# Two weight blocks turned by the DMA crossbar, and a rewritten head, in a convolution with max pooling

## The chip, the cores and the metric

The kernel runs on one core of one Trainium2 chip. The time is device microseconds (us) of an execution. The profile shows one of these executions; its span is about 1.8 us shorter than the time quoted for the same run. Where a run is called slow, it was over 1.5% above the fastest run of the same kernel; ratios and intervals use fast runs alone.

## The reference

A 3x3 convolution with zero padding, followed by a 2x2 maximum. Cut to what matters:

```python
# x: (16, 64, 64, 64) float32, weight: (128, 64, 3, 3) float32, pool_size = 2
conv[b, co] += weight[co, ci, kh, kw] * x_pad[b, ci, kh:kh+h, kw:kw+w]
...
output[b, c, i, j] = max over the 2x2 window of conv[b, c]      # (16, 128, 32, 32) float32
```

## The kernel before

The sixteen images go through in 16 stages, each with a quarter (16 rows of the convolution, 8 of the pooled output) of two "k" images and of two "w" images. Both kinds use the fact that the two rows of a pooling window share a part of their sums: max(u+c, v+c) = max(u,v)+c. Seven combinations of the three weight rows are therefore made from the weights (blocks D2, G0, D0, G2, GM, G1, GP), and turned so that input channels lie on partitions, as TensorE needs them.

The steps have short names. For the k images: PA and PB are twelve products each on the rows themselves (`kx`), PR is six on sums of rows (`ks`) with G1. For the w images: P2 takes differences `we` with GM, P0 takes `wz` with G0, P3 takes `wy` with G2, P1 takes `ws` with GP, six products each. KS, WS, E, Z, Y make these rows (VectorE, or GpSimd for Z and Y). EV, MX, OD and CM copy out and take maxima; SE seeds an accumulator. TX turns block X on TensorE, VX copies it out of PSUM. The number after the point is the stage.

```python
    def turn(m):                                  # four TensorE transposes of one block
        t = free.popleft()
        turned[m] = t
        ...
        for j in range(lo, hi):
            nc.tensor.transpose(tp[...], wq[:, j : j + 2, :].rearrange("a b c -> a (b c)"), ident)

    def turn_out(m):                              # PSUM to the weights in SBUF
        ...
        if m == "GM":
            nc.scalar.mul(dst, src, 0.5)
        elif m == "GP":
            nc.vector.tensor_scalar_mul(out=dst, in0=src, scalar1=0.5)
        elif m in ("G0", "G1", "G2"):
            nc.scalar.copy(out=dst, in_=src)
        else:
            nc.vector.tensor_copy(out=dst, in_=src)
    ...
    def we(i):
        if i < 5:
            inst = on_vector(row_op(nc.vector, "we", i, 1, 0, SUB))
            if i == 0:
                behind(kload(0, chunk(2)[0], H), inst)     # GpSimd load of kx, with a cast
    ...
    def cast_rows(first):                          # XO, XE: kfirst to bf16
        inst = on_vector(nc.vector.tensor_copy(out=kx[0][:, first:khi:2, :], in_=kfirst[...]))
        if first == 1:
            for i in range(1, NQ):
                behind(wload(i), inst)             # SyncE loads wx1, wx2, wx3
    ...
    HEAD = """
        D2 g0 D0 g2 GS g1 TD2 VD2 TG0 VG0 XO TD0 VD0 TG2 VG2 TG1 VG1 XE GM PA.0 GP TGM VGM TGP
        KS.0 E.0 WS.0 PB.0 EV.0 X1 Z.0 Y.0 VGP P2.0 MX.0 SE.0 X2 PA.1 EV.1 WS.1 KS.1 E.1 PR.0
        P0.0 P3.0 Z.1 Y.1 OD.0 CM.0 P2.1 ev.0 PB.1 SE.1 mx.0 P0.1 P1.0 MX.1 P3.1 ev.1 od.0 PR.1
        ...
    """
    for n in range(8):                             # warm-up products on zeros
        warm = zero(n // 2, n % 2)
        if n == 3:
            behind(wload(0), warm)
            nc.sync.dma_start(out=ksecond, in_=rows_of(0, klo2, khi2))
```

Each engine works in the order in which its steps stand in the list. `wload(i)` is the load of the i-th quarter of the first w images; I call these loads wx0 to wx3.

Of the kernel before, what the change touches and what calls it, by code (L numbers as in the profile page):

```python
# [11 lines left out]
def kernel(  # L12
# [21 lines left out]
    nc = tc.nc  # L34
    FP32 = mybir.dt.float32
    BF16 = mybir.dt.bfloat16
    MAX = mybir.AluOpType.max
    ADD = mybir.AluOpType.add
    SUB = mybir.AluOpType.subtract

    B, CI, H, W = x.shape
# [4 lines left out]
    NQ = 4  # L46
# [13 lines left out]

    acc = [psum.tile([128, 2, R, W], FP32, name=f"acc_{i}") for i in range(4)]
    free = deque(range(4))
    unset = set()



# [3 lines left out]
    def behind(inst, other):  # L70
        if other is not None:
            tc.add_manual_dep(inst.ins, other.ins.name, SYNC, reason="order")

    def on_vector(inst):
        sbuf_op[0] = inst
        return inst

    def on_gpsimd(inst):
        behind(inst, sbuf_op[0])
        return inst  # L80


    def rows_of(p, lo, hi):
        return x[2 * p : 2 * p + 2].rearrange("b c h w -> (b c) h w")[:, lo:hi, :]

    def chunk(q):
        return (2 * R * q + (q > 0), min(H, 2 * R * (q + 1) + 1))
# [4 lines left out]
    def kload(j, lo, hi):  # L92
        if j not in kx:
            kx[j] = kx_pool.tile([128, H, W], BF16, name="kx")
        return nc.gpsimd.dma_start(out=kx[j][:, lo:hi, :], in_=rows_of(2 * j, lo, hi))  # L95

    def wload(i):
        j, q = divmod(i, NQ)
        lo, hi = chunk(q)
        return nc.sync.dma_start(  # L100
            out=wx[j % 2][:, lo + 1 : hi + 1, :], in_=rows_of(2 * j + 1, lo, hi)
        )
# [6 lines left out]
    klo2, khi2 = chunk(1)  # L109
    ksecond = const.tile([128, khi2 - klo2, W], FP32)  # L110
# [10 lines left out]
    D2, G0, D0, G2, GM, G1, GP = range(1, 29, 4)  # L121
    BLOCKS = {"D2": D2, "G0": G0, "D0": D0, "G2": G2, "GM": GM, "G1": G1, "GP": GP}
    wq = const.tile([CO, 29, CI], BF16)
    wt = const.tile([128, 28, CO], BF16)
# [4 lines left out]
    g0, g1, g2 = wv[:, 0:3, :], wv[:, 3:6, :], wv[:, 6:9, :]  # L129

    def slots(m):
        return wq[:, m : m + 3, :]

    def zero(t, h):
        return nc.tensor.matmul(  # L135
            acc[t][:, h], zeros[:, 0:128], zeros, start=True, stop=True, skip_group_check=True
        )

    turned = {}

    def turn(m):
        t = free.popleft()
        turned[m] = t
        unset.add(t)
        tp = acc[t][:, 0].rearrange("p a b -> p (a b)").bitcast(BF16)
        lo, hi = BLOCKS[m] - 1, BLOCKS[m] + 3
        for j in range(lo, hi):
            nc.tensor.transpose(  # L148
                tp[:, (j - lo) * 128 : (j - lo + 1) * 128],
                wq[:, j : j + 2, :].rearrange("a b c -> a (b c)"),  # L150
                ident,
            )

    def turn_out(m):
        t = turned[m]
        free.append(t)
        lo, hi = BLOCKS[m] - 1, BLOCKS[m] + 3
        src = acc[t][:, 0].rearrange("p a b -> p (a b)").bitcast(BF16)[:, 0 : (hi - lo) * 128]
        dst = wt[:, lo:hi, :].rearrange("p a b -> p (a b)")
        if m == "GM":  # L160
            nc.scalar.mul(dst, src, 0.5)
        elif m == "GP":
            nc.vector.tensor_scalar_mul(out=dst, in0=src, scalar1=0.5)
        elif m in ("G0", "G1", "G2"):
            nc.scalar.copy(out=dst, in_=src)
        else:
            nc.vector.tensor_copy(out=dst, in_=src)


    def taps(t, m0, rows, start=False, skip=None):  # L170
# [63 lines left out]
    def row_out(name, i):  # L234
        j, q = divmod(i, NQ)
        if (name, j) not in row:
            row[name, j] = row_pool.tile([128, HO, W], BF16, name=name)
        return row[name, j][:, q * R : (q + 1) * R, :]

    def row_in(t, first, pad):  # L240
        a = first + pad
        return t[:, a : a + 2 * R - 1 : 2, :]

    def row_op(engine, name, i, a, b, op):
        j, q = divmod(i, NQ)
        t, pad = (kx[j], 0) if name == "ks" else (wx[j % 2], 1)
        f = 2 * R * q
        return engine.tensor_tensor(  # L248
            out=row_out(name, i), in0=row_in(t, f + a, pad), in1=row_in(t, f + b, pad), op=op
        )  # L250

    def ks(i):
        on_vector(row_op(nc.vector, "ks", i, 0, 1, ADD))

    def ws(i):
        on_vector(row_op(nc.vector, "ws", i, 0, 1, ADD))
# [1 line left out]
    def we(i):  # L258
        if i < 5:
            inst = on_vector(row_op(nc.vector, "we", i, 1, 0, SUB))  # L260
            if i == 0:
                behind(kload(0, chunk(2)[0], H), inst)
        else:
            on_gpsimd(row_op(nc.gpsimd, "we", i, 1, 0, SUB))

# [69 lines left out]
    def cast_rows(first):  # L335
        inst = on_vector(
            nc.vector.tensor_copy(out=kx[0][:, first:khi:2, :], in_=kfirst[:, first:khi:2, :])
        )
        if first == 1:
            for i in range(1, NQ):  # L340
                behind(wload(i), inst)

    def cast_more(first):
        nc.scalar.copy(out=kx[0][:, klo2 + first : khi2 : 2, :], in_=ksecond[:, first::2, :])
# [2 lines left out]
        "g0": lambda: nc.scalar.copy(out=slots(G0), in_=g0),  # L347
        "g1": lambda: nc.scalar.copy(out=slots(G1), in_=g1),
        "g2": lambda: nc.scalar.copy(out=slots(G2), in_=g2),
        "D2": lambda: on_vector(nc.vector.tensor_sub(out=slots(D2), in0=g2, in1=g1)),  # L350
        "D0": lambda: on_vector(nc.vector.tensor_sub(out=slots(D0), in0=g0, in1=g1)),
        "GS": lambda: on_gpsimd(nc.gpsimd.tensor_tensor(out=gsum, in0=g0, in1=g2, op=ADD)),
        "GM": lambda: on_vector(
# [2 lines left out]
        "GP": lambda: on_vector(  # L356
            nc.vector.tensor_add(out=slots(GP), in0=gsum, in1=g1)
        ),
        "XO": lambda: cast_rows(1),
        "XE": lambda: cast_rows(0),  # L360
        "X1": lambda: cast_more(0),
        "X2": lambda: cast_more(1),
        "PA": pa, "PB": pb, "PR": pr, "P0": p0, "P1": p1, "P2": p2, "P3": p3,
        "KS": ks, "WS": ws, "E": we, "Z": wz, "Y": wy, "SE": seed,
        "EV": lambda i, h=None: evac(("k", i), h), "ev": lambda i, h=None: evac(("w", i), h),
        "MX": lambda i, h=None: rowmax(("k", i), h), "mx": lambda i, h=None: rowmax(("w", i), h),
# [3 lines left out]
    for m in BLOCKS:  # L370
        steps["T" + m] = lambda m=m: turn(m)
        steps["V" + m] = lambda m=m: turn_out(m)

    HEAD = """
        D2 g0 D0 g2 GS g1 TD2 VD2 TG0 VG0 XO TD0 VD0 TG2 VG2 TG1 VG1 XE GM PA.0 GP TGM VGM TGP
        KS.0 E.0 WS.0 PB.0 EV.0 X1 Z.0 Y.0 VGP P2.0 MX.0 SE.0 X2 PA.1 EV.1 WS.1 KS.1 E.1 PR.0
        P0.0 P3.0 Z.1 Y.1 OD.0 CM.0 P2.1 ev.0 PB.1 SE.1 mx.0 P0.1 P1.0 MX.1 P3.1 ev.1 od.0 PR.1
        WS.2 KS.2 E.2 Z.2 Y.2 OD.1 cm.0 CM.1 PA.2 EV.2 P2.2 PB.2 SE.2 mx.1 P1.1 P0.2 MX.2 P3.2
        od.1 ev.2 cm.1 E.3 KS.3 WS.3 Z.3 Y.3 PR.2 PA.3 OD.2 CM.2 P2.3 mx.2 EV.3 PB.3 SE.3 P1.2
# [12 lines left out]
    """  # L392
    FIRST, LAST = 4, 12

    for n in range(8):
        warm = zero(n // 2, n % 2)
        if n == 3:
            behind(wload(0), warm)
            nc.sync.dma_start(out=ksecond, in_=rows_of(0, klo2, khi2))
    kx[0] = kx_pool.tile([128, H, W], BF16, name="kx")  # L400

    def run(order):
# [44 lines left out]
```

## Time and profile before

| | before |
|---|---|
| time, median of 4 runs | 107.96 us (107.49 to 108.42) |
| profiled run, its span | 107.78 us, 106.0 us |
| TensorE products | 900: 8 warm-up, 28 transposes, 864 of the convolution |
| second we starts, P2.1 starts, PB.1 starts | 13.04, 13.77, 14.43 us |
| from PB.1 to the end of the block of products | 76.89 us (91.32 - 14.43) |

The page's slices cut the span into 40 parts of 2.65 us. A digit is the busy share in tenths, and PEclk the granted TensorE clock in tenths of full speed:

```profile
PE   5999999999999999999999999999999999999810
PEclk9999999999999999999999999999999999999998
```

TensorE has no hole and, once it is warm, no slice at a lower clock. One thing that the prediction did not show: what leads up to PB.1. The timeline of the head (start, length, engine, line, operation):

```profile
10.95 1.26 POOL L248 TENSOR_TENSOR wy<-wx 128x512 bf16<-128x512 f32 x1
11.10 1.68 DVE L248 TENSOR_TENSOR ws<-wx 128x512 bf16<-128x512 f32 x1
...
13.04 0.68 DVE L248 TENSOR_TENSOR we<-wx 128x512 bf16<-128x512 f32 x1
...
13.64 0.68 DVE L318 TENSOR_TENSOR o<-acc,od 128x512 f32<-128x512 f32 x1
...
14.43 1.46 PE L183 MATMUL acc<-kx,wt 64*128 64x512 bf16 x12
```

VectorE's second `ws` takes 1.68 us beside GpSimd's `wy`, although elsewhere it takes 0.68. The line at 13.64 is CM.0, which frees the accumulator that PB.1 needs. It ends at 14.32 and PB.1, the last line, starts at 14.43. So VectorE, too, runs nearly without slack here.

### The profile page before, as it was taken

The page shows a single profiled execution, that of the slowest core. Times are in us where ns is not written, and L with a number is a line of the kernel's source. Part 1 is how long each engine was busy: PE and PEld are TensorE (multiplying, and loading weights), DVE is VectorE, ACT ScalarE, POOL GpSimd, SP SyncE. Part 2 cuts the span into 40 slices and gives each one's busy share as a digit, 9 for nine tenths or more (in the row PEclk, how much of TensorE's full clock was granted, in tenths as well). Part 3 has the DMA queues.
Part 4 walks back from the last instruction along what each step waited for, and adds up shares of the span by engine and source line. Part 5 has one row for each costly group of instructions (what it writes and reads, how often), then busy time and mean ns, then how long its engine had stood idle before and what let it go on. Part 6 is the DMA issues. An engine that isn't in the chain of part 4 may idle for free.

```text
span 106.0 us, 2338 instructions
## 1 busy us (share of the span) xinstructions
PE 99.5 (94%) x900; PEld 46.0 (43%) x900; DVE 82.4 (78%) x113; ACT 72.8 (69%) x92; POOL 60.1 (57%) x69
## 2 busy tenths in 40 slices
PE   5999999999999999999999999999999999999810
PEld 2465434444444444444444444444444444455400
DVE  1398989979797868697887868687969878677950
ACT  4567985776767678767867676777777676775820
POOL 6205673924529494959567594949294856745000
PEclk9999999999999999999999999999999999999998
DMA  2999976999998569999959498999967412232052
GB/s 58 363 340 359 293 177 153 208 280 244 272 341 192 209 161 152 212 334 210 340 211 212 167 201 148 243 326 202 370 224 158 162 58 102 99 105 99 0 198 99
DMA packets 12475, 21.96 MB, mean 207 GB/s; under 512 B 944, under 2 KB 9136, under 8 KB 12464
## 3 DMA queue, kind: packets, MB, share of 16 engines
q1 hardware_dynamic: 11312, 18.03, 53.7%
q0 software_dynamic: 1008, 3.65, 20.0%
q8 instruction: 7, 0.11, 0.4%
q10 hardware_dynamic: 144, 0.13, 0.4%
q14 instruction: 4, 0.03, 0.1%
HBM read 17.07 MB, written 8.39 MB: 240 GB/s over the span
## 4 chain that ended last, share of the span: by engine, by line
PE 89%; DVE 6%; issue 1%; ACT 1%; DVEq 0%
PE acc L183 83%; DVE acc L299 5%; PE acc L135 3%; PE acc L148 2%; DVE o L318 1%; ACT od L304 1%; DVE zeros L112 0%; DVEq L299 0%
## 5 line engine op out<-in xcount | busy, mean ns | idle before, releaser
L183 PEld LDWEIGHTS <-wt 64*128 64x128 bf16 x864 | 42.6, 94 | 50.8 <-issue 1.1
L299 DVE TENSOR_TENSOR acc<-acc,ev 128x1024 f32<-128x1024 f32 (+1 forms) x34 | 39.6, 1166 | 12.3 <-PE acc L183 12.0
L183 PE MATMUL acc<-kx,wt 64*128 64x504 bf16 (+3 forms) x384 | 46.2, 373 | 0.0
L286 ACT COPY ev<-acc 128x1024 f32<-128x1024 f32 (+1 forms) x34 | 32.6, 964 | 12.5 <-PE acc L183 11.0
L248 POOL TENSOR_TENSOR wz<-wx 128x512 bf16<-128x512 f32 x16 | 20.4, 1273 | 30.2 <-DVE ws L248 23.3
L304 ACT COPY od<-acc 128x512 f32<-128x512 f32 x32 | 18.8, 587 | 11.5 <-PE acc L183 11.5
L318 DVE TENSOR_TENSOR o<-acc,od 128x512 f32<-128x512 f32 x32 | 21.9, 690 | 3.6 <-ACT od L304 3.6
L248 POOL TENSOR_TENSOR wy<-wx 128x512 bf16<-128x512 f32 x16 | 20.3, 1268 | 0.0
L295 ACT ACTIVATE acc<-acc 128x1024 f32<-128x1024 f32 x16 | 16.1, 1008 | 1.0 <-PE acc L183 0.6
L248 POOL TENSOR_TENSOR we<-wx 128x512 bf16<-128x512 f32 x11 | 14.0, 1276 | 0.1
L183 PE MATMUL acc<-ws,wt 64*128 64x504 bf16 (+1 forms) x96 | 13.0, 377 | 0.4 <-DVE acc L299 0.4
L183 PE MATMUL acc<-ks,wt 64*128 64x504 bf16 (+1 forms) x96 | 13.0, 377 | 0.1
L183 PE MATMUL acc<-we,wt 64*128 64x504 bf16 (+1 forms) x96 | 13.0, 377 | 0.0
L183 PE MATMUL acc<-wy,wt 64*128 64x504 bf16 (+1 forms) x96 | 13.0, 377 | 0.0
L183 PE MATMUL acc<-wz,wt 64*128 64x504 bf16 (+1 forms) x96 | 13.0, 377 | 0.0
L248 DVE TENSOR_TENSOR ws<-wx 128x512 bf16<-128x512 f32 x16 | 12.0, 747 | 0.0
L248 DVE TENSOR_TENSOR ks<-kx 128x512 bf16<-128x512 bf16 x16 | 6.7, 416 | 0.0
L95 POOL DMA_DIRECT2D kx<-in_x_dram x7 | 4.1, 591 | 3.5 <-DVE we L248 3.5
L135 PE MATMUL acc<-zeros 128*128 128x512 bf16 x8 | 3.6, 631 | 1.2 <-DVE zeros L112 1.2
L248 DVE TENSOR_TENSOR we<-wx 128x512 bf16<-128x512 f32 x5 | 3.4, 682 | 0.0
L148 PEld LDWEIGHTS <-wq 128*128 128x128 bf16 x28 | 2.4, 124 | 1.0 <-issue 0.6
L148 PE MATMUL acc<-ident,wq 128*128 128x128 bf16 x28 | 2.6, 265 | 0.0
(26 smaller groups left out, 14.9 us busy)
## 6 DMA issues: line engine op xcount, KB each, us to landing
out_dram<-o SPq DMA_DIRECT2D x31, 256.0 KB, 2.8
wx<-in_x_dram SPq DMA_DIRECT2D x8, 512.0 KB, 5.6
wx<-in_x_dram SPq DMA_DIRECT2D x4, 544.0 KB, 5.7
kx<-in_x_dram POOLq DMA_DIRECT2D x4, 496.0 KB, 7.7
wx<-in_x_dram SPq DMA_DIRECT2D x4, 480.0 KB, 4.7
kx<-in_x_dram POOLq DMA_DIRECT2D x3, 528.0 KB, 8.1
kfirst<-in_x_dram SPq DMA_DIRECT2D x1, 544.0 KB, 4.3
ksecond<-in_x_dram SPq DMA_DIRECT2D x1, 512.0 KB, 5.7
```

Source lines behind the costliest of these rows:

```text
L95: return nc.gpsimd.dma_start(out=kx[j][:, lo:hi, :], in_=rows_of(2 * j, lo, hi))
L135: return nc.tensor.matmul(acc[t][:, h], zeros[:, 0:128], zeros, start=True, stop=True, skip_group_check=True)
L148: nc.tensor.transpose(tp[:, (j - lo) * 128 : (j - lo + 1) * 128], wq[:, j : j + 2, :].rearrange("a b c -> a (b c)"), ident,)
L183: nc.tensor.matmul(dst[:, half, i0:i1, o0:o1], wt[lo : lo + CI, m0 + kw - half, :], rows(lo, i0, i1, c0, c1), start=start and kw == 1, sto ...
L248: return engine.tensor_tensor(out=row_out(name, i), in0=row_in(t, f + a, pad), in1=row_in(t, f + b, pad), op=op)
L286: nc.scalar.copy(out=ev[g][:, halves(h)], in_=acc[ta[g]][:, halves(h)])
L295: nc.scalar.mul(acc[t], acc[ta["w", i]], -1.0)
L299: nc.vector.tensor_tensor(out=t, in0=t, in1=ev[g][:, halves(h)], op=MAX)
L304: nc.scalar.copy(out=od[g][:, halves(h)], in_=acc[tb[g]][:, halves(h), :, 1::2])
L318: nc.vector.tensor_tensor(out=o, in0=acc[tb[g]][:, s, :, 0::2], in1=od[g][:, s], op=MAX)
```

## The change

The intent: take eight of the 28 weight transposes off TensorE (blocks G1 and GP) and give them to the DMA crossbar, which writes into the weights directly; start the convolution earlier with two warm-up products fewer; and issue each load only when its turn in the order of need has come, so that early loads have the DMA engines to themselves.

```diff
+    def turn_by_dma(m):
+        lo = BLOCKS[m] - 1
+        for j in (lo, lo + 1):
+            nc.sync.dma_start_transpose(
+                out=wt[:, j : j + 3 : 2, :], in_=wq[:, j : j + 4, :].rearrange("a b c -> a (b c)")
+            )
 ...
     def ks(i):
-        on_vector(row_op(nc.vector, "ks", i, 0, 1, ADD))
+        inst = on_vector(row_op(nc.vector, "ks", i, 0, 1, ADD))
+        if i == 0:
+            behind(kload(0, chunk(2)[0], H), inst)
 ...
             inst = on_vector(row_op(nc.vector, "we", i, 1, 0, SUB))
             if i == 0:
-                behind(kload(0, chunk(2)[0], H), inst)
+                for n in range(2, NQ):
+                    behind(wload(n), inst)
 ...
-        if first == 1:
-            for i in range(1, NQ):
-                behind(wload(i), inst)
+        if first == 0:
+            behind(wload(1), inst)
 ...
     HEAD = """
-        D2 g0 D0 g2 GS g1 TD2 VD2 TG0 VG0 XO TD0 VD0 TG2 VG2 TG1 VG1 XE GM PA.0 GP TGM VGM TGP
-        KS.0 E.0 WS.0 PB.0 EV.0 X1 Z.0 Y.0 VGP P2.0 MX.0 SE.0 X2 PA.1 EV.1 WS.1 KS.1 E.1 PR.0
+        D2 g0 D0 g2 GS g1 XG1 TD2 VD2 TG0 VG0 XO TD0 VD0 TG2 VG2 GM XE PA.0 TGM GP HGP XGP KS.0
+        PB.0 EV.0 VGM E.0 WS.0 X1 P2.0 Z.0 Y.0 SE.0 MX.0 X2 PA.1 EV.1 E.1 KS.1 WS.1 PR.0
         P0.0 P3.0 Z.1 Y.1 OD.0 CM.0 P2.1 ev.0 PB.1 SE.1 ...
-    for n in range(8):
+    for n in range(6):
```

Cut from the diff: ksecond's load now waits for the first difference block; all four accumulators start on the list of untouched ones, which have to be zeroed before they are seeded (e1 meets this); GM's scaling moves from ScalarE to VectorE (VGM, 0.42 us); GP is halved by ScalarE before it is turned (HGP). XG1 and XGP are two crossbar transposes each, issued by SyncE.

> **What bounds the kernel now.** I read the page's busy table first, then the chain that ended last in order of time, then the timeline of the first 22 us on every engine, then the DMA issues. The busy table, and the chain:
>
> ```profile
> PE 99.5 (94%) x900; PEld 46.0 (43%) x900; DVE 82.4 (78%) x113; ACT 72.8 (69%) x92; POOL 60.1 (57%) x69
> ```
>
> ```profile
> 0.86 0.28 DVE zeros L112
> ...
> 1.19 3.59 PE acc L135 x8
> 4.79 1.77 PE acc L148 x20
> 6.56 1.32 PE acc L183 x12
> 7.88 0.55 PE acc L148 x8
> 8.44 5.30 PE acc L183 x48
> 13.74 0.03 issue
> 13.77 77.56 PE acc L183 x720
> ```
>
> The columns are start, length and what ran. TensorE (PE) is the chain from 1.19 to 91.3 us almost without a hole. 720 convolution products take 77.56 us, 0.1077 us each, so all 864 need 93.05 us and cannot be shortened by this change. What is left of the 106.0 us span is 13 us: a head before 6.56 us (eight warm-up products, 3.59 us, and 20 transposes of weights), eight more transposes (0.55 us) and a tail after 91.3 us. The change touches the head only; steady state and tail have the same order of work. A microsecond saved on TensorE in the head is a microsecond of the run, if the later inputs also come that much earlier.
>
> The timeline of the head shows which inputs come just in time (start, length, what, and in brackets the idle time before it):
>
> ```profile
> 3.71 0.50 DVE L350 TENSOR_TENSOR wq<-wraw 128x192 bf16<-128x192 f32 x1 [2.57 <-DMA wraw<-in_weight_dram]
> ...
> 5.59 0.42 DVE L337 CAST kx<-kfirst 128x512 bf16<-128x512 f32 x1
> ...
> 6.04 1.28 SPq L100 DMA_DIRECT2D wx<-in_x_dram  x3
> ...
> 6.49 1.39 PE L183 MATMUL acc<-kx,wt 64*128 64x512 bf16 x12
> ...
> 8.00 0.68 DVE L248 TENSOR_TENSOR we<-wx 128x512 bf16<-128x512 f32 x1
> ...
> 9.68 0.81 PE L183 MATMUL acc<-we,wt 64*128 64x512 bf16 x6
> ...
> 11.62 0.82 PE L183 MATMUL acc<-ks,wt 64*128 64x512 bf16 x6
> ...
> 13.77 1.63 PEld L183 LDWEIGHTS <-wt 64*128 64x128 bf16 x18 [0.52 <-DVE we L248]
> ...
> 16.41 0.81 PE L183 MATMUL acc<-ws,wt 64*128 64x512 bf16 x6
> ```
>
> To be seen: the weights arrive at 3.71 us; the first difference block is ready at 4.21, just before the warm-up ends. The rows are cast at 5.59, done at 6.01, but the first convolution starts only at 6.49, because TensorE still transposes. The product with G1 (ks) starts at 11.62 and that with GP (ws) at 16.41: these are the two dates that a transpose by DMA has to meet. At 13.77 the weight load had been idle 0.52 us for a VectorE result.
>
> ```profile
> wx<-in_x_dram SPq DMA_DIRECT2D x8, 512.0 KB, 5.6
> ...
> kfirst<-in_x_dram SPq DMA_DIRECT2D x1, 544.0 KB, 4.3
> ksecond<-in_x_dram SPq DMA_DIRECT2D x1, 512.0 KB, 5.7
> ```
>
> The last column is us from issue to landing. kfirst, issued at 1.19, lands at 5.5; ksecond, issued at 3.48, at 9.2. From 2.6 to 10.6 us the page's slices show 340 to 363 GB/s: the head's loads are limited by transfer, not by issue.
>
> **What the Trainium skill says.** (1) "VectorE: DVE Perf Modes", section "The three transpose paths": a 128x128 bf16 transpose takes 390 ns on TensorE and 1309 ns through the DMA crossbar. The trace has no DMA transpose; the 28 TensorE ones have a mean of 265 ns but overlap, 20 in 1.98 us and the last 8 in 0.62 us. (2) "DMA: Bandwidth & Descriptors", section "Queues, rings and completion order": descriptors of a ring are consumed in ring order. So a transpose issued by SyncE behind ksecond cannot overtake it, and wx1 issued behind the transposes cannot overtake these. ksecond, issued 2.3 us after kfirst and landing 3.7 us after it, with wx0 between them, agrees. (3) "TensorE: Matmul & The Clock Gate", Part 1: TensorE runs at half clock until one observation window of some 3.4 us was busy. The trace agrees: the weight loads of the zero products start 0.43 us apart, twice the 0.215 us that two overlapping convolution products take; the transposes speed up from 5 starts per 0.25 us to 7 only at about 6.0 us.
>
> **The change part by part.**
>
> 1. Two warm-up products fewer. They are 0.43 us apart, so the warm-up ends about 0.86 us earlier. But the first block is ready at 4.21, so the transposes can start near 4.3 instead of 4.58: 0.3 us, the rest becomes idle.
> 2. TG1's four transposes leave TensorE ahead of the first convolution. At 1.98/20 = 0.099 us each that is 0.4 us. Together with (1), transposes end near 4.3 + 16 x 0.099 = 5.9 instead of 6.56. Now the cast rows bind: kfirst lands at 5.5, the cast takes 0.42 and ends near 6.0, so the first convolution starts near 6.05. Gain 0.44 us, not 0.7.
> 3. TGP's four transposes go: half of the 0.55 us, 0.28 us. Running gain 0.72 us.
> 4. VectorE and ScalarE are reshuffled: ScalarE loses the 0.59 us copy of G1 and the 0.60 us scaling of GM, and gains a halving of GP in its place (about 0.55 us, as the casts of the same 128x192 size). VectorE keeps one scaling of 0.42 us, now of GM and ahead of the first we. Working along the new order with the old durations: first convolution 6.05 to 7.35, TGM to 7.65, PB.0 to 9.0, VectorE's ks 8.0, GM scaled 8.4, we 9.1; P2.0 starts near 9.15 (before 9.68), PA.1 near 9.95 (ScalarE: halving, eviction, then the cast of ksecond at about 9.25), PR.0 near 11.25 (before 11.62), P2.1 near 13.2 (before 13.77). About 0.15 us of the 0.72 is lost to waits on we and on the cast: gain 0.57 us.
> 5. Added: four crossbar transposes on SyncE, each 128x256 bf16, 64 KB, two 128x128 blocks. As bytes they are nothing: 256 KB at 350 GB/s is 0.7 us of transfer in all. At the skill's 1309 ns per block they are 2.6 us each and 10.5 us together, an estimate that takes the blocks as serial. G1's pair is issued at about 5.2 (its cast ends at 5.1) and GP's when its halving ends near 8.2. G1 has to land by 11.25, GP by about 15.8.
> 6. Loads gated later: wx1 at the second cast (7.2 us, or when SyncE is free) instead of 6.04; wx2 and wx3 after the first we, near 9.1. wx1 has to land by about 12.4 so that its we (0.68 us) is done at 13.2.
>
> In the good case all of 5 and 6 is hidden: ksecond's bytes are through at about 8, the G1 pair adds a few tenths, wx1 takes 1.5 us at 350 GB/s plus completion and lands at 11 to 12. Sum: 107.57 - 0.57 = 107.0 us.
>
> **The rivals.** (a) *The transposes are slow.* At 2.6 us each, one after the other from 5.2, the G1 pair is done at 10.4 and lands near 11.4: 0.15 us late. wx1, if SyncE is held until then, is issued at 10.4 and lands at about 13.9; P2.1 follows at 14.65, 1.4 us behind plan and 0.9 behind before. GP's pair would hold SyncE to about 16, wx2 lands near 19.5 and costs perhaps another 0.8 us: total 107.57 + 1.7 = 109.3. Were SyncE held still longer, 3.5 us per transpose, the same sum gives about 111. Against: in the new order G1's product has six us from issue to use, and gating wx1 and wx2 behind the transposes looks as if their cost was known. (b) *The clock rises later.* With a hole of about half a us at 3.8 and another before the first convolution, a busy window may be missed. Until the next one, up to 3.4 us later, products take twice as long: up to 1.7 us lost, total 108.7. Against: before, the rise came at about 6.0, after 4.8 us of work, and 16 transposes still fill most of the time. The run of 108.35 among three shows that the head can vary by 0.8 us. (c) *The saving is hidden anyway*: if ksecond, not TensorE, sets PA.1, the gain is eaten there. ksecond's cast started at 9.64 before, 0.4 us after landing, so at most half of the gain can go: total 107.3.
>
> **Range and chances.** The good case is 107.0; rival (c) and small waits for wx1 make 107.1 the likeliest. Below: 0.8 us would need the full 0.72 and the hole at 13.7 gone, 106.3. Above: (a) at 2.6 us, or (b), gives 108.7 to 109.3, so 109.0 as upper edge. Over 2% faster means under 105.4, a gain of 2.1 us, three times what leaves TensorE: 0.02. Over 2% slower means over 109.7, which takes rival (a) at over 2.6 us per transpose, or (a) and (b) together: 0.12. Within 2%: 0.86.
>
> **What the changed profile would show.** Right: 890 TensorE products (900 before), 20 of them transposes; the first convolution near 6.05; the ks product near 11.2 with no wait on a DMA; P2.1 near 13.2; the block of 720 products again 77.6 us, ended 0.5 to 0.6 earlier; tail equal. Wrong by (a): SyncE's transposes with microseconds each, TensorE waiting for a DMA into wt, or VectorE's we waiting for wx1. Wrong by (b): the first twelve convolution products taking well over 1.32 us. Wrong by (c): PA.1 waiting for the cast of ksecond. What I cannot read from this profile is the duration of a crossbar transpose and how long it holds SyncE; the whole upper half of the range is that.

## The result, and the profile after

The changed kernel took **112.56 us**, the median of 4 runs (111.66 to 113.94; the run of 113.94 counts as slow), against 107.96 before. The ratio of the fast runs is 1.0399, with an interval of 1.0297 to 1.0501: slower by 4%. A ratio is the mean time of one kernel's fast runs over that of the other's of the same rounds, so it is not quite the ratio of the quoted medians. The result was correct. 112.56 lies 3.6 us above the upper edge of the predicted range.

The busy line and the slices of the page after:

```profile
PE 99.8 (90%) x890; PEld 49.0 (44%) x890; DVE 81.5 (73%) x113; ACT 72.1 (65%) x91; POOL 60.1 (54%) x69
...
PE   5887907999999999999999999999999999999920
...
PEclk9999997699999999999999999999999999999998
```

To be seen: 890 products as planned; the sixth slice (13.9 to 16.7 us) is empty on TensorE; and in slices 7 and 8 the granted clock falls to 0.7 and 0.6, long after the warm-up. The chain that ended last, in order of time (start, length, what):

```profile
7.77 8.21 DMA wx<-in_x_dram
16.01 0.04 DVE we L254
...
17.64 0.61 DVE o L327
18.25 0.04 issue
18.29 78.49 PE acc L189 x714
```

Where TensorE was almost the whole chain before, a load of 8.21 us is now part of it. It is wx1. The timeline of the head (the bracket is the idle time before the instruction and what ended it):

```profile
5.13 2.60 SPq L171 DMA_TRANSPOSE wt<-wq  x2
...
6.04 1.39 PE L189 MATMUL acc<-kx,wt 64*128 64x512 bf16 x12 [0.59 <-DVE kx L346]
...
7.77 0.58 SPq L100 DMA_DIRECT2D wx<-in_x_dram  x1
...
8.18 0.70 POOL L95 DMA_DIRECT2D kx<-in_x_dram  x1 [2.73 <-DVE ks L254]
8.22 0.68 DVE L254 TENSOR_TENSOR we<-wx 128x512 bf16<-128x512 f32 x1
8.39 2.91 SPq L171 DMA_TRANSPOSE wt<-wq  x2
...
10.45 1.47 PE L189 MATMUL acc<-kx,wt 64*128 64x512 bf16 x12 [0.63 <-ACT kx L355]
...
11.75 0.83 PE L189 MATMUL acc<-ks,wt 64*128 64x512 bf16 x6
...
16.01 0.69 DVE L254 TENSOR_TENSOR we<-wx 128x512 bf16<-128x512 f32 x1 [5.36 <-DMA wx<-in_x_dram]
...
16.76 0.82 PE L189 MATMUL acc<-we,wt 64*128 64x512 bf16 x6 [2.88 <-DVE we L254]
...
18.29 2.74 PE L189 MATMUL acc<-kx,wt 64*128 64x512 bf16 x12 [0.71 <-DVE o L327]
```

Reading down: SyncE issues the first transposes at 5.13, each holding it 1.3 us, and then wx1 at 7.77, the GpSimd load of `kx` starts at 8.18, and the second pair of transposes at 8.39. wx1 lands at 15.98. VectorE waits 5.36 us for it with the second `we` (P2.1's rows), and TensorE waits 2.88 us for that. PB.1, the next block of twelve, takes 2.74 us instead of 1.46. It cannot start before CM.0 (`o`, line 327), which stands behind that `we` in VectorE's order.

The stretches of one us show both losses. The columns after the stretch are its length, the busy time (and count) of PE, PEld, DVE, ACT and POOL, then the granted clock, the DMA share and GB/s:

```profile
9.00:10.00 1.00, 0.82 (x8) 0.30 (x6) 1.00 (x2) 0.22 (x1) 0.35 (x1) 1.00 0.83 131
...
14.00:15.00 1.00, 0.00 (x0) 0.00 (x0) 0.00 (x0) 0.38 (x1) 0.00 (x0) 1.00 2.65 138
...
19.00:20.00 1.00, 1.00 (x8) 0.39 (x6) 0.38 (x1) 0.00 (x0) 1.00 (x1) 0.50 1.06 350
```

Between 9 and 10 us the DMA engines are busy (share 0.83) and yet move 131 GB/s, where the kernel before moved 385 GB/s in the same stretch, and e4 (below: the same waits, but plain copies in place of the transposes) 272 GB/s at a share of 0.82. In the second line the durations of the packets even add up to 2.65 times the engines' time; I read from it only that packets took long while little was moved. Between 19 and 20 us TensorE is never idle, but at half clock.

The sum from the two traces: PB.1 starts at 18.29 instead of 14.43, 3.86 us later. The 714 products from there take 78.49 instead of 76.89 us, 1.60 us more. After the last maximum the end of the program comes 0.36 us sooner (3.15 instead of 3.51 us, the last store). 3.86 + 1.60 - 0.36 = 5.10, and the spans differ by 111.1 - 106.0 = 5.1 us. So two things are to be explained: why wx1 takes 8.2 us, and why 714 products cost 1.6 us more.

### The profile page after: what moved, and what is told of

Read it like the earlier page. It is cut to its first block, busy times and chain, and to the rows that moved or that the text cites. A ratio compares the mean times of both kernels' runs of the same rounds, so it can differ in the third digit from the quotient of the medians.

```text
span 111.1 us, 2322 instructions
## 1 busy us (share of the span) xinstructions
PE 99.8 (90%) x890; PEld 49.0 (44%) x890; DVE 81.5 (73%) x113; ACT 72.1 (65%) x91; POOL 60.1 (54%) x69
## 3 DMA queue, kind: packets, MB, share of 16 engines
q1 hardware_dynamic: 12464, 18.29, 56.6%
HBM read 17.07 MB, written 8.39 MB: 229 GB/s over the span
## 4 chain that ended last, share of the span: by engine, by line
PE 75%; DMA 11%; DVE 9%; issue 1%; ACT 1%; SPq 0%; DVEq 0%
PE acc L189 75%; DMA wx<-in_x_dram 7%; DVE acc L308 5%; DMA kfirst<-in_x_dram 4%; DVE o L327 1%; DVE kx L346 1%; DVE ks L254 1%; DVE ws L254 1%; ACT od L313 1%; DVE wq L367 0%; SPq L105 0%; DVE wq L370 0%; DVE wt L166 0%; DVEq L308 0%; DVE we L254 0%
## 5 line engine op out<-in xcount | busy, mean ns | idle before, releaser
L189 PEld LDWEIGHTS <-wt 64*128 64x128 bf16 x864 | 47.0, 95 | 53.2 <-issue 5.6
L189 PE MATMUL acc<-kx,wt 64*128 64x504 bf16 (+3 forms) x384 | 47.7, 381 | 1.9 <-DVE o L327 0.7
L189 PE MATMUL acc<-wz,wt 64*128 64x504 bf16 (+1 forms) x96 | 13.6, 386 | 0.0
L254 DVE TENSOR_TENSOR ws<-wx 128x512 bf16<-128x512 f32 x16 | 11.0, 685 | 0.0
L135 PE MATMUL acc<-zeros 128*128 128x512 bf16 x6 | 2.7, 630 | 1.2 <-DVE zeros L112 1.2
L362 DVE TENSOR_TENSOR wq<-wraw 128x192 bf16<-128x192 f32 x1 | 0.5, 499 | 2.5 <-DMA wraw<-in_weight_dram 2.5
L365 POOL TENSOR_TENSOR gsum<-wraw 128x192 f32<-128x192 f32 x1 | 0.8, 828 | 2.3 <-DVE wq L364 2.3
```

The source lines that it names most:

```text
L135: return nc.tensor.matmul(acc[t][:, h], zeros[:, 0:128], zeros, start=True, stop=True, skip_group_check=True)
L189: nc.tensor.matmul(dst[:, half, i0:i1, o0:o1], wt[lo : lo + CI, m0 + kw - half, :], rows(lo, i0, i1, c0, c1), start=start and kw == 1, sto ...
L254: return engine.tensor_tensor(out=row_out(name, i), in0=row_in(t, f + a, pad), in1=row_in(t, f + b, pad), op=op)
L362: on_vector(nc.vector.tensor_sub(out=slots(D2), in0=g2, in1=g1))
L365: "GS": lambda: on_gpsimd(nc.gpsimd.tensor_tensor(out=gsum, in0=g0, in1=g2, op=ADD)),
```

## The experiments

**My theory** after the traces: the crossbar transposes, in flight together with ordinary loads, slow these on the DMA engines that they share; the hole that this leaves makes the clock fall. **The rivals**: the new gating issues wx1 too late (7.77 instead of 6.04 us) and the crossbar is innocent; SyncE is held too long; any small extra transfer at that place would do the same; the clock falls for a reason of its own. A first set undoes one part at a time on one chip.

### e1: all of the change except the crossbar

Both blocks are turned by TensorE again; the rest of the new head stays.

```diff
-        elif m in ("G0", "G2"):
+        elif m in ("G0", "G1", "G2"):
-  ... g1 XG1 TD2 ... VG2 GM XE PA.0 TGM GP HGP XGP KS.0
+  ... g1 TD2 ... VG2 TG1 VG1 GM XE PA.0 TGM GP TGP KS.0
-  ... WS.0 X1 P2.0 ...
+  ... WS.0 X1 VGP P2.0 ...        # VGP scales by 0.5 on VectorE, as before
```

> The changed head, but G1 and GP turned by TensorE again (TG1, VG1, TGP, VGP back), six warm-ups and the new gates kept. Theory X (the crossbar transposes delay wx1): wx1 lands by about 12, no TensorE hole of microseconds, no half clock, 107.0 to 107.6 us. Rival L (the late gate of wx1 and the earlier kx load alone delay wx1): wx1 still lands near 15 to 16, 111 us or more.

Measured: 108.27 us median (fast runs 108.04, 108.11, 108.42; one slow), ratio 1.0016 (0.9938 to 1.0093): same. wx1, issued at 7.32, landed at 12.46, and P2.1 started at 13.92. So the gating costs little, and the 4% come with the crossbar. One confounder: in this order the seeding step met an untouched accumulator and zeroed it with two products (0.54 us of the chain). A later run removes it.

### e2 and e3: one pair by crossbar

e2 gives only G1 to the crossbar, e3 only GP. Both edits are halves of e1's.

```diff
 e2:  g1 XG1 TD2 ... VG2 GM XE PA.0 TGM GP TGP KS.0 ... X1 VGP P2.0
 e3:  g1 TD2 ... VG2 TG1 VG1 GM XE PA.0 TGM GP HGP XGP KS.0 ... X1 P2.0
```

> Only G1 by the crossbar, GP by TensorE; wx1 is issued behind the G1 pair. Theory X with the pair ahead of wx1 to blame: wx1 lands at 14 to 16, 110 to 112 us. Theory X with the pair behind wx1 (GP) to blame: wx1 lands at 11.5 to 13, 107 to 108 us.

> Only GP by the crossbar, G1 by TensorE; wx1 is issued with no transpose ahead of it, near 7.3 us. Pair ahead to blame: wx1 lands at 11 to 12.5, 107 to 108 us. Pair behind to blame (its packets stall the engines beside wx1's): wx1 lands at 14 to 16, 110 to 112 us.

Measured: e2 had fast runs of 108.51 and 108.09 and slow ones of 112.71 (the profiled one) and 109.74; ratio 1.0026 (0.9925 to 1.0126). e3 had fast runs of 111.56 and 110.26 and slow ones of 112.5 (profiled) and 113.37; ratio 1.0267 (1.0145 to 1.0389), unclear at the 2% line. In the profiled runs wx1 landed at 15.64 and 16.23. A repeat of e2 for one look, on another chip:

> e2_g1_dma (G1 alone by the crossbar) profiled again: its times lay at 108.1 to 112.7 and the profile fell on the longest. If the same kernel sometimes meets the stall and sometimes not: wx1 lands either near 12.5 with some 108 us, or near 15.6 with 110 or more. If G1's pair always delays wx1: near 15.6 again.

It took 109.53 us, wx1 landed at 14.14. So one pair is enough to delay wx1, and the delay differs from run to run. With "slow" defined by time alone, such runs may be called slow because of the delay itself, as the two profiled ones show it; their traces may say what happened inside them, not how much slower the kernel is. In e3, wx1 was issued at 7.01, before any transpose (7.88), and still took 9.2 us. That speaks against the order of issue and against SyncE being held.

### e4: the same bytes, not transposed

Plain copies of the same 64 KB take the place of the transposes, same places, same waits. The result is wrong on purpose.

```diff
-            nc.sync.dma_start_transpose(
-                out=wt[:, j : j + 3 : 2, :], in_=wq[:, j : j + 4, :].rearrange("a b c -> a (b c)")
-            )
+            nc.sync.dma_start(
+                out=wt[:, j : j + 3 : 2, :],
+                in_=wq[:, j : j + 4, :].rearrange("a (b c) d -> a b (c d)", c=2),
+            )
```

> Wrong result on purpose: the four crossbar transposes become four plain copies of the same 64 KB between the same tiles, issued at the same places with the same gates. Theory X in its crossbar form: SyncE is held about 0.4 us each instead of 1.3, wx1 lands by about 12, 107 us. Rival S (any small-packet copies in the ring do it): wx1 near 15 to 16, 111 to 113 us.

Measured: fast runs 107.49, 107.59, 107.81, one slow; ratio 0.997 (0.9872 to 1.0069): same. In the trace of e4, first the timeline, then the chain:

```profile
12.27 0.69 DVE L255 TENSOR_TENSOR we<-wx 128x512 bf16<-128x512 f32 x1 [1.35 <-DMA wx<-in_x_dram]
```

```profile
14.56 76.86 PE acc L190 x714
```

wx1 landed at 12.25 after 5.19 us, and the 714 products took 76.86 us. Against this kernel the changed one starts PB.1 3.73 us later and needs 1.63 us more for the 714 products: 5.36, and the spans differ by 111.1 - 105.7 = 5.4 us. So the whole loss hangs on these four transfers being transposes; their bytes, the gating and the order, which e4 keeps, cost nothing measurable. SyncE was held 0.68 us by a copy against 1.30 by a transpose, which moves wx1's issue by 0.7 us only, from 7.06 to 7.77.

### e5: the hole filled, to separate the clock

Products on zeros are put ahead of P2.1, so that TensorE works while it waits for wx1.

```diff
         t = ta["w", i] = free.popleft()
+        if i == 1:
+            for n in range(13):
+                zero(t, n % 2)
         taps(t, GM, step1(row["we", i // NQ], i % NQ), start=True)
```

> The changed kernel with thirteen products of zeros (0.215 us each at full clock, 2.8 us) put on TensorE just ahead of P2.1, where the changed kernel's TensorE sat idle for 2.9 us; they write P2.1's own bank, which P2.1's first product then overwrites. Theory H (the idle hole makes the clock fall to half for 3.4 us, and that is 1.7 of the loss): no half clock after the hole, about 110.5 to 111.2 us against 112.2 to 112.9. Rival (the half clock is no cost of its own, the later part waits for data anyway): 112 to 113 us.

Measured: fast runs 111.51, 110.22, 110.88; ratio 1.0265 (1.0195 to 1.0334). The profiled run (111.89, just over the line and called slow) had wx1 even later, at 16.63. Timeline, then chain:

```profile
13.84 2.98 PE L135 MATMUL acc<-zeros 128*128 128x512 bf16 x12
```

```profile
18.94 76.86 PE acc L189 x714
```

The hole is filled, and the 714 products take 76.86 us as in e4: no half clock, with PB.1 later than in the changed kernel. So the half clock is a consequence of the hole, and worth 1.63 us. The mean granted clock of the fast runs, recorded for each, agrees: 0.990 to 0.999 here, 0.977 to 0.981 in the changed kernel. Other traces fit, with one limit: after a hole of 2.56 us (e2), 3.39 (e3) or 2.28 (e11, below) there was half clock, after one of 0.75 us (e2 repeated) the 714 products took 76.86. But holes of 1.50 us (e7), 1.88 (e13) and 2.12 (e6 repeated) left the clock full as well, so not every hole does it. Whether the length alone decides, or also where the hole lies in time, no run tests.

### e6: wx1 issued ahead of the transposes

```diff
-        if first == 0:
-            behind(wload(1), inst)
         behind(nc.sync.dma_start(out=ksecond, in_=rows_of(0, klo2, khi2)), inst)
+        wload(1)
```

wx1 is issued right behind ksecond.

> The changed kernel with wx1 issued right behind ksecond, ahead of G1's transposes, everything else the same. Theory X-ring (wx1 is late because it queues behind and beside the crossbar packets): wx1 lands at 10.5 to 11.5, G1's pair at 12 to 14, so the hole moves to the G1 product and is smaller: 108 to 109.5 us. If the crossbar's packets also hold back what is issued ahead of them: wx1 lands after 13 and the time stays above 110.

The profiled run took 269.45 us: TensorE's products averaged some 0.82 us over the whole span, instead of 0.377. Its trace holds no record of the granted clock, so that the clock was low is not shown. The other runs were 114.71 and 115.14 (slow) and 109.73 (fast). I have no explanation, and a single fast run gives no ratio. The repeat on another chip:

> e6_wx1_first once more, since its profiled run fell into a state in which TensorE never got past a fraction of its clock (267.7 us span). If wx1 ahead of the crossbar packets is out of their reach: it lands at 10.5 to 12.5. The G1 pair, now behind wx1 and beside GpSimd's kx load, then lands at 13 to 15 and the G1 product waits for it: 109 to 112 us. If neither waits: 107.5 to 108.5.

It had fast runs of 108.94, 108.58 and 109.67 and two slow ones (the profiled one and 112.47); ratio 1.0097 (1.0014 to 1.018). In its profiled run (111.22, slow) wx1 landed at about 11.97, in time because it was issued at 4.55, though it was under way for 7.4 us (7.8 in e6); but one of G1's transposes only at 15.60, and the product with G1 waited 2.4 us for it. The loss had moved from one load to another. The `kx` load had again started beside the transposes, at 7.95.

### e7 and e12: the GpSimd load moved away from the crossbar

e7 moves the load of `kx` behind the second `we`, e12 behind the first `wz` (at 11.0 us). The crossbar stays.

```diff
     def ks(i):
-            behind(kload(0, chunk(2)[0], H), inst)       # at i == 0
 e7: def we(i):
+            if i == 1:
+                behind(kload(0, chunk(2)[0], H), inst)
 e12: def wz(i):
+        inst = on_gpsimd(row_op(nc.gpsimd, "wz", i, -1, 1, SUB))
+        if i == 0:
+            behind(kload(0, chunk(2)[0], H), inst)
```

> The changed kernel with GpSimd's load of the remaining kx rows (496 KB) gated behind the second we, which itself waits for wx1, in place of the first ks; the transposes stay. Theory C (the crossbar packets alone hold back wx1): wx1 still lands at 14 to 16 and the time stays at 111 to 113. Rival K (only the crossbar together with GpSimd's queue on the same engines holds back wx1): wx1 lands at 11 to 12.5, 107 to 108.5 us.

> The changed kernel with GpSimd's kx load moved by some 2.7 us, right behind the first wz (10.9 us). Theory (crossbar and GpSimd's queue must meet to hold back wx1): with wx1 nearly through by then, it lands at 12 to 13.5 and the later kx load at 17.5 to 19; 108 to 110 us, between e7 and the changed kernel. If it lands near 16 again: any overlap suffices, 111 to 113.

Measured: e7 had fast runs of 109.98 and 109.33, ratio 1.0152 (1.0085 to 1.0219), and slow ones of 113.10 and 111.79, as long as the changed kernel's and not profiled, so what happened in them is not known; e12 four fast runs from 109.35 to 110.08, ratio 1.0161 (1.0099 to 1.0222). Both are unclear at the 2% line. The timeline of e7's head:

```profile
12.72 0.69 DVE L254 TENSOR_TENSOR we<-wx 128x512 bf16<-128x512 f32 x1 [2.22 <-DMA wx<-in_x_dram]
```

wx1 lands at 12.70 (e12: 12.53), nearly as with plain copies, though it stands between the same four transposes and was issued at 7.86. So in these two profiled runs the crossbar alone does not delay it; it takes the load of the second queue beside it. What remains of 1.5% is another wait: the rows of `kx`, loaded late, land at 20.5 (e12: 19.90) and TensorE waits for them. That wait is the experiment's own: e13 below, with no transpose and the same late load (landed 20.55), waits 1.88 us for these rows and takes 110.18 us. Taking e7's 1.5% for the price of the crossbar would be wrong.

### e9: transpose and copy alone

In the kernel before, four transposes and then four plain copies of 64 KB were added at the very end, into scratch tiles, where no load is under way any more; only the last two output stores still were, until 105.08 us, beside the first transpose (103.10 to 105.52).

```diff
     run(TAIL)
+    for n in range(4):
+        nc.sync.dma_start_transpose(out=scrx[...], in_=wq[...])   # the first waits for the last maximum
+    for n in range(4):
+        nc.sync.dma_start(out=scrp[...], in_=wq[...])
```

> The kernel before with four crossbar transposes and then four plain copies of the same 64 KB, from the weights to scratch tiles, issued after the last output, where the engines have nothing else to do. Only their own figures count. If the crossbar is slow by itself: 3 to 6 us from issue to landing against about 2 for a plain copy. If it is slow only under load: about 2 to 3 us each for both, with SyncE held 1.2 to 1.3 us by a transpose and about 0.6 by a copy.

From the list of DMA issues (out<-in, size where given, us from issue to landing):

```profile
scrp<-wq SPq DMA_DIRECT2D x4, 64.0 KB, 2.0
...
scrx<-wq SPq DMA_TRANSPOSE x4, 2.3
```

So, with no load beside it, a transpose of two 128x128 blocks lands 2.3 us after issue, a copy after 2.0. A transpose held SyncE 1.29 us (5.15 for four), a copy 0.84. In the changed kernel such transposes took 4.0 to 8.8 us to land; but the plain copies in the same places (e4) took 4.1 to 7.6, so this difference comes mostly from what else is under way, not from the crossbar. This was a single run of 115.94 us, so only these durations count.

### e11 and e13: is it GpSimd, or any second queue?

In e7's kernel, ScalarE issues a load of the same rows, without cast and into a tile that nobody reads, where GpSimd's load was. e13 is the same with plain copies for the transposes (wrong on purpose).

```diff
+        if i == 0:                                        # in ks
+            behind(nc.scalar.dma_start(out=spare, in_=rows_of(0, chunk(2)[0], H)), inst)
```

> As e7_kload_late, with an extra load of the same rows issued by ScalarE at the place where the changed kernel had GpSimd's load, into a spare tile that nobody reads (no cast, 992 KB). Only wx1's landing counts (12.7 in e7, 16.0 in the changed kernel). If any second queue beside the crossbar packets holds back wx1: 15 us or later. If it is GpSimd's queue in particular: 12.7 to 14.

> Wrong result on purpose: e11_act_load with plain copies in place of the crossbar transposes, the control that e11 lacks. Only wx1's landing counts (15.05 in e11). If ScalarE's extra load alone took the bandwidth: 14 to 15.5. If crossbar and second queue must meet: 11.5 to 13.5.

One run each, on different chips: 113.19 and 110.18 us. The second `we`, in e11:

```profile
15.07 0.69 DVE L255 TENSOR_TENSOR we<-wx 128x512 bf16<-128x512 f32 x1 [4.26 <-DMA wx<-in_x_dram]
```

and in e13:

```profile
12.20 0.69 DVE L256 TENSOR_TENSOR we<-wx 128x512 bf16<-128x512 f32 x1 [1.71 <-DMA wx<-in_x_dram]
```

With the crossbar and ScalarE's load, wx1 lands at 15.05; with plain copies and the same load, at 12.17. So neither GpSimd nor the cast is special: transposes beside a load of another queue are. The single packets do not show this split: the longest of the small ones (256 bytes; median 18 ns) took 18 ns in e13 and 31 ns in e4, where nothing is transposed, but 2.05 us in the changed kernel, 0.95 in e11 and also 1.15 in e7 and 1.03 in e12, where no second queue loads and wx1 is in time. Slow packets come with the transposes; wx1 is late only where a second load is there too.

### The runs side by side

One line for each kernel of the set that issues wx1 at 7.0 to 8.0 us, from the profiled run of each; the last column is us from issue to landing of wx1.

| kernel | crossbar | second queue's load beside it | wx1 issued, landed | us |
|---|---|---|---|---|
| e1 | none | GpSimd | 7.32, 12.46 | 5.1 |
| e4 | none (plain copies) | GpSimd | 7.06, 12.25 | 5.2 |
| e13 | none (plain copies) | ScalarE | 7.00, 12.17 | 5.2 |
| e7 | both pairs | none | 7.86, 12.70 | 4.8 |
| e12 | both pairs | none until 11.0 | 7.73, 12.53 | 4.8 |
| e2 repeated | G1 | GpSimd | 8.00, 14.14 | 6.1 |
| e11 | both pairs | ScalarE | 7.82, 15.05 | 7.2 |
| e2 | G1 | GpSimd | 7.78, 15.64 | 7.9 |
| changed kernel | both pairs | GpSimd | 7.77, 15.98 | 8.2 |
| e5 | both pairs | GpSimd | 7.85, 16.63 | 8.8 |
| e3 | GP | GpSimd | 7.01, 16.23 | 9.2 |

Where one of the two is missing, wx1 takes 4.8 to 5.2 us (4.5 in e1b below, from 7.10 to 11.59); where both are there, 6.1 to 9.2. e6 and its repeat, which issue wx1 at 4.6 and have both, fit with 7.8 and 7.4. The landings with one missing hardly differ between chips, so I take the split as shown, although e11, e13 and the repeat of e2 are single runs.

### e1b, e10, e15: why no gain even without the crossbar

e1 and e4 gain nothing, although TensorE has less to do in e4. e1b is e1 without the two zeroing products (VGM moved ahead of EV.0). e10 is e1b with the load gates of before for wx1 to wx3 and `kx`. e15 is e1b with ksecond and wx1 issued as early as before, and `kx` behind the first `we` as before; wx2 and wx3 stay behind that `we` too.

```diff
 e1b: -PB.0 EV.0 VGM E.0 WS.0 ...   +PB.0 VGM EV.0 E.0 WS.0 ...
 e10, e15: kload behind the first we, wload(1..3) behind XO or the first we
 e15: +nc.sync.dma_start(out=ksecond, in_=rows_of(0, klo2, khi2))   # at the fourth warm-up product
```

> As e1_tensor (all weight blocks by TensorE, the changed head's warm-ups and gates), but with the copy of GM ahead of the first eviction in the order, so that no tile has to be zeroed by two products (0.54 us in e1_tensor). If those two products were all that kept the new head from gaining: P2.1 starts near 13.4 and the time is 107.1 to 107.6 us, 0.2 to 0.6 under before. If the new head gains nothing at all: 107.7 to 108.3.

> A try for a better version than both: as e1b_clean, but with the gates of the kernel before (wx1 to wx3 at the first cast, the kx load behind the first we). wx1 lands near 10.5 again, P2.1 near 13.2; 107.0 to 107.4 us. If the head is bound by something else: 107.6 or more.

> A second try for a better version: e1b_clean (all transposes on TensorE) with ksecond issued as early as before (3.5 us), wx1 at the first cast, and kx, wx2, wx3 behind the first we. If the head is bound by when ksecond and wx1 land: ksecond near 9.2, wx1 near 10.5, P2.1 near 13.3, 107.0 to 107.5 us. If it is bound by VectorE's and TensorE's order: 107.6 to 108.2.

Measured: ratios 1.0005 (0.9934 to 1.0077), 1.0063 (1.0011 to 1.0116), 1.0057 (0.9993 to 1.012), all "same". None is faster than before, and the traces show three different reasons. In e1b the clock became full only at 7.12 us (the first twelve products took 1.63 us instead of 1.39), and later P2.2, the same step a stage on, waited for wx2 (landed 18.29): it began at 20.59, before at 19.66. In e10 PA.1 waited for the cast of ksecond (landed 10.55 instead of 9.19) and began at 11.24 instead of 10.32. In e15 no load was late up to PB.1, and VectorE is the limit. The timeline of e15:

```profile
10.85 2.11 DVE L254 TENSOR_TENSOR we<-wx 128x512 bf16<-128x512 f32 x1
11.13 1.27 POOL L254 TENSOR_TENSOR wy<-wx 128x512 bf16<-128x512 f32 x1
...
14.55 1.47 PE L189 MATMUL acc<-kx,wt 64*128 64x512 bf16 x12 [0.58 <-DVE o L326]
```

wx1 landed in time here (10.44). But the second `we`, as the `ws` before, runs beside GpSimd's `wy` and takes 2.11 us instead of 0.68, and PB.1 waits for CM.0 behind it: 14.55, against 14.43 before. The first convolution started 0.41 us earlier (6.08 against 6.49), and nothing of it was left at PB.1. The Trainium skill describes such a conflict ("SBUF — State Buffer", section "SBUF: two separate sides"): VectorE operations with two SBUF inputs and GpSimd operations share a port pair, and the later one waits for the whole of the earlier. The durations agree: 2.11 (e15), 1.78 (e1b), 1.70 (e10) and 1.68 us (before) beside `wy`, 0.68 otherwise.

### e16 and e17: two tests of that chain

e16 drops the second `we` and reads the first one's rows again (wrong on purpose). e17 gives GM's scaling back to ScalarE, which takes 0.42 us out of VectorE's way ahead of the first `we`. Both start from e15.

```diff
 e16: +        if i == 1:
      +            return                     # in we
      -        taps(t, GM, step1(row["we", i // NQ], i % NQ), start=True)
      +        taps(t, GM, step1(row["we", i // NQ], 0 if i == 1 else i % NQ), start=True)
 e17: +        if m == "GM":
      +            nc.scalar.mul(dst, src, 0.5)
```

> Wrong result on purpose: e15_loads without VectorE's second we (2.1 us there, 0.7 elsewhere, run beside GpSimd's wy); P2.1 reads the first we instead. If the chain we, ws (VectorE), wz, wy (GpSimd), second we, ks, ws, first output (VectorE) sets the start of PB.1, PB.1 starts near 13.6 instead of 14.55 and the time falls by 0.7 to 1.0 us against e15_loads, to some 107.3. If loads or TensorE set it: PB.1 near 14.5 and about 108.2.

> Third try for a better version, right result: e15_loads with GM scaled by ScalarE as in the kernel before, so that the first we on VectorE starts some 0.4 us earlier. If that chain sets the head: first we near 7.8, PB.1 near 14.1, 107.2 to 107.7 us. If not: as e15_loads, 107.9 to 108.3.

Measured: e16 had four fast runs from 107.6 to 107.9, ratio 0.9965 (0.9925 to 1.0005); PB.1 started at 14.12. The timeline of e16, then its chain:

```profile
14.12 1.47 PE L189 MATMUL acc<-kx,wt 64*128 64x512 bf16 x12
```

```profile
9.34 8.50 DMA kx<-in_x_dram
...
18.89 0.61 DVE o L328
19.50 0.04 issue
19.55 71.67 PE acc L189 x666
```

So with the operation gone, PB.1 moves 0.43 us: VectorE did hold it in e15. But the expectation was 13.6 and 0.7 to 1.0 us less than e15, and only half of it came. The chain now runs through the `kx` load, which lands at 17.84, and P2.2 begins at 19.55, against 19.73 in e15 and 19.66 in the kernel before. The profiled spans are 105.9 (e16), 106.1 (e15) and 106.0 us (before), and the ratio of 0.9965 (some 0.4 us) has an interval that reaches 1. So VectorE's order is one limit, and the `kx` load the next one behind it; freeing the first alone wins nothing clear. e17 had fast runs of 107.61, 107.39, 108.54, 108.89 and 108.33, ratio 1.0002 (0.9953 to 1.0051): the move of GM alone gives nothing. Its profiled run was a slow one (109.53), in which the clock rose late: its first twelve convolution products took 2.58 us instead of 1.39. That is rival (b) of the prediction, seen in this run and not in the changed kernel's.

No version beat the kernel before clearly; e16 and e4, the two with a ratio below 1, give wrong results.

## Why the prediction was right or wrong

- **First convolution (steps 1 and 2): right.** Predicted near 6.05, measured 6.04, waiting for the cast rows as said. Before, it was 6.49.
- **G1 in time, PR.0 without a wait for a DMA: right.** The pair landed at 10.26 and 10.44 and was needed at 11.75. GP's pair landed at 17.15 and 17.37, 1.4 to 1.6 us after my date of 15.8; its product came only at 21.87.
- **PA.1 (rival (c)): half right.** It waited 0.63 us for the cast of ksecond and started at 10.45 instead of the 9.95 of step 4. In the changed kernel this half microsecond lies ahead of the wait for wx1 and is hidden by it.
- **The failed step: "In the good case all of 5 and 6 is hidden", with "wx1 takes 1.5 us at 350 GB/s plus completion and lands at 11 to 12".** wx1 took 8.2 us from issue and landed at 15.98. I had costed the transposes as bytes and as a hold on SyncE, and not as something that slows other transfers. With plain copies in their place wx1 landed at 12.25 (e4), and with the second queue's load moved away at 12.70 and 12.53 (e7, e12). The "1.5 us plus completion" was too short in any case: even in e4 wx1 was under way for 5.19 us.
- **Rival (a): right place, wrong mechanism.** It said that VectorE's `we` would wait for wx1. But it let SyncE be held 2.6 us per transpose and wx1 be issued at 10.4. SyncE was held 1.3 us, wx1 was issued at 7.77, and the delay lay in the transfer. So the size came out too small: P2.1 at 14.65 as against 16.76.
- **Rival (b): right effect, wrong place.** I expected half clock at the start only. The start cost nothing in the changed run (the first twelve products took 1.39 us), but the hole at 13.9 to 16.76 us cost 1.63 us of half clock at 18.22 to 21.63. A wait was priced at its length; it also had an aftermath.
- **Step 4's gain of 0.57 us: wrong, and independent of the crossbar.** I followed the new order to P2.1 and took what was won there for the win of the run. PB.1, two steps on, hangs on VectorE's order (first `we`, `ws`, then GpSimd's `wz` and `wy`, the second `we`, CM.0), and there nothing was won: 14.55 in e15 and 14.56 in e4, against 14.43 before. (In e15 it waits at `wy` and the second `we`; in e4 the second `we` waits for wx1.) "The block of 720 products again 77.6 us" failed with it.
- **Sums and readings that were off, without bearing on the result.** "0.8 us would need the full 0.72 and the hole at 13.7 gone" adds up to 0.72 + 0.52 = 1.24 us, which is what 106.3 stands for. GP's halving took 0.36 us, not 0.55. The upper edge of 109.0 lay below the 109.3 of rival (a) itself. That a transfer behind another in SyncE's queue "cannot overtake" it is more than the cited section says, which speaks of the order in which descriptors are taken up; in the traces here the loads and transposes of SyncE in the head did land in their order of issue.
- **The chances**: 0.86 for "within 2%" rested on the gating looking "as if their cost was known". That is an argument about an author's intent, not a reading of the profile. I also wrote that the duration of a crossbar transpose could not be read from the profile; that doubt deserved a wider range.

Still open: how transposes and loads hold each other up inside the DMA engines (the runs show that they do, not how); why it varies so between executions; what the run of 269.45 us was; whether the same extra load on SyncE's own queue, and not on a second one, would delay wx1 as well, which no run tried; and whether the transposes would be harmless if all of them were done before any second queue loads, for which the weights come too late here.

## What to carry to other kernels

A DMA that costs few bytes can still be dear: before giving work to the crossbar, list which loads of other queues are in flight at the same time, and compare with a plain copy of the same bytes to see what the crossbar itself does. Price a hole on TensorE at its length plus the half clock that may follow it, and fill it with products on zeros where it cannot be removed. And follow a gain in the head through every engine's order up to the point from which TensorE is the chain, not only to the next product.

## What the Trainium skill lacked or had wrong

- "DMA: Bandwidth & Descriptors", section "Rules for kernel authors", says that a transpose next to ordinary DMAs "needs nothing". The rule is about results, and for these it held: every run that was not wrong on purpose was correct. Of time it says nothing, and a reader may take it for both: beside crossbar transposes and a second queue's load, wx1 landed at 15.98 us; with plain copies at 12.25; with the second load moved away at 12.70. The transposes themselves landed 4.0 to 8.8 us after issue, and plain copies in their places 4.1 to 7.6; with no load beside them it was 2.3 and 2.0.
- "VectorE: DVE Perf Modes", section "The three transpose paths", gives 1309 ns for one 128x128 block on the crossbar. Here an instruction of two blocks held SyncE 1.29 us and landed after 2.3 us with no load beside it; that section says nothing of how long the issuing engine is held.
- "TensorE: Matmul & The Clock Gate", section "Why this matters for your kernels", advises against gaps of more than some 3 us. Here a hole of 2.28 us (e11) and one of 2.88 us (changed kernel, with a further 0.71 us before PB.1) were enough; after the latter the clock was halved for 3.41 us. Holes of 2.12 us (e6 repeated) and 1.88 us (e13) left it full. A further idle time of 0.71 us alone does nothing: e5 and the repeat of e2 had it too, at full clock. The same page (Part 1) tells of a clock seen stuck for 50 us and more; here one execution (e6) had products of 0.82 us instead of 0.377 over its span of 267.7 us; its trace holds no record of the clock, so whether it is the same state is not shown.
